# Position biases by an indirect DMA of rows in place of one-hot products

## The chip, the cores and the metric

The kernel runs on one core of a Trainium2 chip. The metric is the device time of one execution in microseconds (us); of several runs the median is given.

## The reference, cut to what matters

The program is two transformer blocks over 512 tokens of width 1024, in float32. The first has two layers with three kinds of attention (differential, forgetting, stick-breaking). The second has three branches (sparse attention with an index score, a gated recurrence, attention with low-rank keys) and a feed-forward part. The change touches one input of the sparse attention: a bias for each query, key and head, taken from a table of 32 buckets by the distance of two positions.

```python
def t5_bucket(dist):
    max_exact = REL_BUCKETS // 2
    d = jnp.maximum(dist, 0)
    dl = jnp.maximum(d, max_exact).astype(jnp.float32)
    large = max_exact + (jnp.log(dl / max_exact) / math.log(REL_MAX_DIST / max_exact)
                         * (REL_BUCKETS - max_exact)).astype(jnp.int32)
    large = jnp.minimum(large, REL_BUCKETS - 1)
    return jnp.where(d < max_exact, d, large)
...
        bias = rel_bias[t5_bucket(pb[:, :, None] - p_sel)]
        s = (jnp.einsum('bthd,btkd->bthk', qb, k_sel).astype(jnp.float32) * scale
             + jnp.moveaxis(bias, -1, 2).astype(jnp.float32))
```

The positions are read from an input; from a distance of 113 on all distances fall into the last bucket, and negative ones into the first.

## The kernel before, in words

A class `Net` issues everything; tiles are 128 partitions (P) by up to 512 columns (S), and the 512 tokens are four tiles (NT). Matrix products of full precision are done as three products of high and low parts: weights come by SP's queue into `wraw` (three buffers), ScalarE makes the high part `whi` (L189), VectorE the low part `wlo` (L190), and `mm3` (L197 to L199) issues the three products for each step into a bank `pj` of PSUM. A second kind of bank, `s`, has three buffers, which attention scores and the bias work share.

The biases do not depend on the activations. `bias2` computes them during the first layer of the first block and writes them to DRAM (`bias0` to `bias3`, one for each tile of queries); the sparse attention reads them back much later. It is a Python generator: each `yield` ends a step. `merge` and `merging` run one and a half of its steps for each step of the main sequence (`RATES[7]`, `RATES[8]`), first beside the projections of the values, queries and keys (four, two and two tiles), then beside two pairs of gate tiles; what is left is issued after them. The attention `att_b`, which is issued at a raised priority, runs beside the gates and what follows. A planner then orders the instructions of each engine by priority, program order and its own idea of when each is ready. Each engine, and each queue that issues DMAs (SP, POOL), then keeps that order.

`bias2` works by residues. Positions are taken modulo 256. For a residue of the query and one of the key the table `t5tab` gives the bias of their distance. For each head:

- `raw` reads, for each of the 256 key residues, a shifted row of the table from DRAM (SP's queue, L983) into a buffer `bo`, and `split` (L1032 ScalarE, L1033 VectorE) makes its high and low parts;
- products with the one-hot matrix `ok` of the keys' residues (L990) pick the columns: the result has a row for each of the 256 query residues and a column for each of the 512 keys, in two banks, each of which is split again into high and low parts `g`;
- for each tile of queries, products with the one-hot matrix `oq` of the queries' residues (L998) pick the rows, 128 to 512 columns wide, as keys after the tile are masked anyway;
- L1000 fills a tile `o` (again a buffer `bo`) with the bias of far distances, L1001 copies the picked values over it where the distance is near, and POOL writes it to DRAM (L1002).

`near` and `side`, masks that tell where a distance is near and which sign it has, are made once on VectorE, before the heads. The buffers are shared by tag: `bt` (six of 128x512), `bh` (four, the one-hot matrices) and `bo` (three, for table rows and outgoing biases alike). When `bias2` is done its memory goes to the buffers `lt`, in which the next projections' queries and keys are put (L643 to L646); the copies of L646 run on POOL.

Of the kernel before, what the change touches and what calls it, by code (L numbers as in the profile page):

```python
# [9 lines left out]
F32 = mybir.dt.float32  # L10
F32R = mybir.dt.float32r
# [3 lines left out]
ALU = mybir.AluOpType  # L15
# [4 lines left out]
P = 128  # L20
S = 512
# [12 lines left out]
class Net:  # L34
# [30 lines left out]
    def slot(self, dt=F32, shape=None):  # L65
        return self.u("t2k", shape or [P, S], self.nslot, dt)
# [846 lines left out]
    def bias2(self, pool):  # L913


        nc, a = self.nc, self.a
# [3 lines left out]
        hot = lambda: pool.tile([P, S], F32R, name=self.nm("bh"), tag="bh", bufs=4)  # L920
# [5 lines left out]
        col = self.t("b_col", [P, 4], 1)  # L926
# [26 lines left out]
        ok, oq = ([hot() for _ in range(2)] for _ in range(2))  # L953
        for j in range(2):
            nc.vector.tensor_scalar(ok[j], m, col[:, j:j + 1], None, op0=ALU.is_equal)
            nc.vector.tensor_scalar(oq[j], m, col[:, 2 + j:3 + j], None, op0=ALU.is_equal)
        yield
        ka = part(pi, ALU.arith_shift_right, 7, slot())
# [21 lines left out]
        for h in range(4):  # L980
            raw = pool.tile([P, 2, 256], F32, name=self.nm("bo"), tag="bo", bufs=3)
            x = tab[h]
            nc.sync.dma_start(raw, bass.AP(x.tensor, x.offset, [[1, P], [P, 2], [1, 256]]))  # L983
            f = self.split(raw.rearrange("p a b -> p (a b)"), slot)
            g = []
            for r in range(2):
                ps = self.p("s")
                for k, y in enumerate((0, 0, 1, 1)):
                    z = k % 2
                    nc.tensor.matmul(ps, lhsT=f[y][:, z * 256 + r * P:z * 256 + r * P + P], rhs=ok[z], start=k == 0, stop=k == 3)  # L990
                g.append(self.split(ps, slot))
            yield
            for i in range(NT):
                w = (i + 1) * P
                ps = self.p("s")[:, :w]
                for k, y in enumerate((0, 0, 1, 1)):
                    z = k % 2
                    nc.tensor.matmul(ps, lhsT=oq[z][:, i * P:w], rhs=g[z][y][:, :w], start=k == 0, stop=k == 3)  # L998
                o = pool.tile([P, S], F32, name=self.nm("bo"), tag="bo", bufs=3)[:, :w]
                nc.vector.tensor_scalar(o, side[i], te[:, 1, h:h + 1], te[:, 0, h:h + 1], op0=ALU.mult, op1=ALU.add)  # L1000
                nc.vector.copy_predicated(o, near[i].bitcast(U32), ps)  # L1001
# [706 lines left out]
def constants():  # L1708
# [36 lines left out]
    cc = np.arange(P, dtype=np.float32)[:, None] * [1, 1, -1, -1] + [0, 128, 255, 127]  # L1745
# [28 lines left out]
```

## Time and profile before

| | us |
|---|---|
| median of 3 runs | 1699.47 (1699.45 to 1704.51) |
| the profiled execution's own time | 1701.74 |
| its span in the profile | 1700.0 |
| TensorE busy | 1632.7 |
| VectorE busy | 1074.4 |
| ScalarE busy | 731.2 |
| GpSimd (POOL) busy | 124.9 |

The profile is of one execution. PE is TensorE's matmul, PEld its weight load, DVE is VectorE, ACT is ScalarE, POOL is GpSimd, SP is the engine that issues most DMAs; a letter q behind the name is that engine's instruction queue. Matmuls overlap each other in the record, so the busy time of a group is longer than the time in which the engine issues it; the distance between two starts gives the latter. A line such as L998 is the line of the kernel. In rows of waits the right side names what came last. The granted clock is the share of TensorE's full clock that the throttle let through.

### The profile page before, as it was taken

To read this page: it belongs to the slowest core of one execution; us is meant where nothing else is said; L and a number is where in the kernel's file an instruction comes from. 1 tells how busy PE (TensorE), PEld (TensorE's weight loads), DVE (VectorE), ACT (ScalarE), POOL (GpSimd) and SP (SyncE) were. 2 spreads that over 40 slices of the span, in tenths; PEclk is the share of its full clock that TensorE was granted. 3 is DMA by queue.
4 is the path that set the end of the run, shared out by engine and by line. 5 is a ranking of instruction groups with operands and counts; after the bars stand their busy time and mean duration, and the time that the engine had idled before them with its cause. 6 is when DMAs were issued, how large, how long until landed. Compare 5 with 4: busy or idle time off the path is not lost.

```text
span 1700.0 us, 24423 instructions
## 1 busy us (share of the span) xinstructions
PE 1632.7 (96%) x9384; PEld 1387.3 (82%) x9384; DVE 1074.4 (63%) x2363; ACT 731.2 (43%) x1484; POOL 124.9 (7%) x135
## 2 busy tenths in 40 slices
PE   7999999989999999799889999999999999999997
PEld 6877788878787979688778976788889988888997
DVE  7855878865657787855999996633445544443233
ACT  4434755434556643455443954522333322222222
POOL 2111000020000000201231000200000000000000
PEclk9999999999999999899999999999999999999999
DMA  6331123243121323432012230232523533332221
GB/s 219 109 101 46 38 87 91 84 125 100 38 75 36 115 74 109 133 89 89 13 33 69 64 102 4 90 100 87 173 81 125 186 99 99 99 97 90 96 89 65
DMA packets 140156, 153.79 MB, mean 90 GB/s; under 512 B 13908, under 2 KB 130916, under 8 KB 140040
## 3 DMA queue, kind: packets, MB, share of 16 engines
q1 hardware_dynamic: 134808, 139.24, 26.7%
q0 software_dynamic: 2368, 7.67, 1.3%
q10 hardware_dynamic: 2864, 5.32, 1.0%
q8 instruction: 74, 1.21, 0.3%
q14 instruction: 42, 0.34, 0.1%
HBM read 139.36 MB, written 13.12 MB: 90 GB/s over the span
## 4 chain that ended last, share of the span: by engine, by line
PE 79%; DVE 14%; ACT 3%; DMA 2%; issue 2%; POOL 0%; ACTq 0%; DVEq 0%; SPq 0%; POOLq 0%
PE pj L197 19%; PE pj L199 19%; PE pj L198 19%; PE pv L1022 3%; PE s L199 2%; PE s L198 2%; PE s L197 2%; PE tr L666 2%; PE s L652 1%; PE s L769 1%; PE s L653 1%; DVE ixs L1239 1%; DVE wlo L190 1%; ACT whi L189 1%; DVE tok L286 1%
## 5 line engine op out<-in xcount | busy, mean ns | idle before, releaser
L198 PE MATMUL pj<-hTl,whi 128*128 128x512 f32 (+1 forms) x1136 | 440.6, 388 | 0.0
L197 PE MATMUL pj<-hTh,whi 128*128 128x512 f32 (+1 forms) x1136 | 440.5, 388 | 0.0
L199 PE MATMUL pj<-hTh,wlo 128*128 128x512 f32 (+1 forms) x1136 | 440.0, 388 | 0.0
L190 DVE TENSOR_TENSOR wlo<-wraw,whi 128x1024 fp32r<-128x1024 f32 (+1 forms) x235 | 269.3, 1152 | 236.5 <-ACT whi L189 234.8
L189 ACT CAST whi<-wraw 128x1024 fp32r<-128x1024 f32 (+3 forms) x245 | 237.2, 982 | 354.9 <-PE pj L198 188.8
L197 PEld LDWEIGHTS pj<-hTh,whi 128*128 128x128 f32 x1136 | 213.8, 188 | 45.0 <-issue 6.3
L198 PEld LDWEIGHTS pj<-hTl,whi 128*128 128x128 f32 x1136 | 213.8, 188 | 43.4 <-issue 4.4
L199 PEld LDWEIGHTS pj<-hTh,wlo 128*128 128x128 f32 x1136 | 213.8, 188 | 43.2 <-issue 3.8
L199 PE MATMUL pj<-whi,hTl 128*128 128x256 f32 (+2 forms) x416 | 121.7, 295 | 2.4 <-DVE hTl L263 2.4
L197 PE MATMUL pj<-whi,hTh 128*128 128x256 f32 (+2 forms) x416 | 120.9, 292 | 0.9 <-ACT hTh L262 0.9
L198 PE MATMUL pj<-wlo,hTh 128*128 128x256 f32 (+2 forms) x416 | 121.0, 292 | 0.0
L198 PE MATMUL pj<-wlo,t2k 128*128 128x256 f32 x304 | 85.7, 282 | 0.0
L199 PE MATMUL pj<-whi,t2k 128*128 128x256 f32 x304 | 85.5, 281 | 0.0
L197 PE MATMUL pj<-whi,t2k 128*128 128x256 f32 x304 | 85.3, 281 | 0.0
L199 PEld LDWEIGHTS pj<-whi,hTl 128*128 128x128 f32 x416 | 81.6, 197 | 3.5 <-DVE hTl L263 3.1
L197 PEld LDWEIGHTS pj<-whi,hTh 128*128 128x128 f32 x416 | 81.9, 197 | 2.0 <-ACT hTh L262 1.8
L198 PEld LDWEIGHTS pj<-wlo,hTh 128*128 128x128 f32 x416 | 82.1, 198 | 0.4 <-DVE wlo L190 0.2
L199 PE MATMUL s<-whi,t2k 128*128 128x256 f32 x264 | 73.8, 280 | 0.0
L197 PE MATMUL s<-whi,t2k 128*128 128x256 f32 x264 | 73.8, 280 | 0.0
L198 PE MATMUL s<-wlo,t2k 128*128 128x256 f32 x264 | 73.8, 280 | 0.0
L669 ACT COPY wa<-tr 128x128 f32<-128x128 f32 (+3 forms) x96 | 40.7, 424 | 59.3 <-PE tr L666 57.7
L657 DVE CUSTOM_DVE_ANT_0 wa<-s,mask 128x128 f32<-128x128 f32 (+3 forms) x112 | 52.3, 485 | 14.2 <-PE tr L666 7.6
(441 smaller groups left out, 3081.3 us busy)
## 6 DMA issues: line engine op xcount, KB each, us to landing
wraw<-in_w_in_dram SPq DMA_DIRECT2D x112, 512.0 KB, 3.8
wraw<-in_w_ffn_gate_dram SPq DMA_DIRECT2D x22, 512.0 KB, 4.6
wraw<-in_w_ffn_up_dram SPq DMA_DIRECT2D x22, 512.0 KB, 4.7
wraw<-in_w_ffn_down_dram SPq DMA_DIRECT2D x16, 512.0 KB, 4.4
tok<-hres SPq DMA_DIRECT2D x12, 512.0 KB, 7.4
wraw<-in_w_out_dram SPq DMA_DIRECT2D x12, 512.0 KB, 3.5
hres<-tok SPq DMA_DIRECT2D x12, 512.0 KB, 2.9
wraw<-in_w_out_dram SPq DMA_DIRECT2D x8, 384.0 KB, 3.0
```

Of the source, the lines that this page charges most:

```text
L189: nc.scalar.copy(hi[:, ka:kb], raw)
L190: (eng or nc.vector).tensor_sub(lo[:, ka:kb], raw, hi[:, ka:kb])
L197: nc.tensor.matmul(out, lhsT=wh(k), rhs=xh(k), start=start and k == 0, stop=False)
L198: nc.tensor.matmul(out, lhsT=wh(k), rhs=xl(k), start=False, stop=False)
L199: nc.tensor.matmul(out, lhsT=wl(k), rhs=xh(k), start=False, stop=stop and k == nk - 1)
L286: nc.vector.scalar_tensor_tensor(y, y, mv[:, 2:3], g[half], op0=ALU.add, op1=ALU.mult)
L652: nc.tensor.matmul(sc, lhsT=stacked[:, rows], rhs=twice[hh][:, cols], start=True, stop=False)
L653: return nc.tensor.matmul(sc, lhsT=stacked[:, rows], rhs=twice[2 + hh][:, cols], start=False, stop=stop)
L657: self.nc.vector.tensor_tensor_reduce(p[:, :w], sc[:, :w], self.maskw[:, S - w:] if mask is None else mask, scale=1.0, scalar=3e38, op0=AL ...
L666: x = nc.tensor.transpose(pt[:, j, :], src[:, j * P:(j + 1) * P], self.ident)
L669: nc.scalar.copy(dst[:, :n, :], pt[:, :n, :])
L1022: x = self.nc.tensor.matmul(out, lhsT=l, rhs=r, start=k == 0, stop=k == i)
```

## The change

The one-hot matrix `oq` of the queries and its products (L998) go, and so does the second split. The 256 rows of all four heads are copied from PSUM by ScalarE as they are and written to a DRAM tile `rows` (256 x 4 x 512) by SP's queue. For this, the four heads' first products are issued ahead of the `near` and `side` masks. For each tile of queries, an indirect DMA on POOL's queue then fetches, for each of its 128 queries, that query's row of 4 x 512 values (8 KB) into a buffer `bq`, of which there is one. The predicated copies read from it. The loop over heads is now inside the loop over tiles. Row indices are two operations on small integers: 255 minus the position modulo 256.

```diff
--- before.py
+++ after.py
@@ -913,17 +913,19 @@
     def bias2(self, pool):
 
 
+
         nc, a = self.nc, self.a
         U32 = mybir.dt.uint32
         self.bias = [self.dr.tile([P, 4, (i + 1) * P], F32, name=f"bias{i}") for i in range(NT)]
         slot = lambda dt=F32, shape=None: pool.tile(shape or [P, S], dt, name=self.nm("bt"), tag="bt", bufs=6)
-        hot = lambda: pool.tile([P, S], F32R, name=self.nm("bh"), tag="bh", bufs=4)
+        hot = lambda: pool.tile([P, S], F32R, name=self.nm("bh"), tag="bh", bufs=2)
+        rows = self.dr.tile([256, 4, S], F32, name="t5rows")
         pos = a["positions_2"]
         pi = slot(I32)
         nc.sync.dma_start(pi, pos.broadcast_to([P, S]))
         qi = self.t("b_qi", [P, 3, NT], 1, I32)
         nc.sync.dma_start(qi[:, 0], pos[0].rearrange("(t p) -> p t", p=P))
-        col = self.t("b_col", [P, 4], 1)
+        col = self.t("b_col", [P, 2], 1)
         nc.sync.dma_start(col, a["c_col"])
         rb = self.t("b_rb", [32, 4], 1)
         nc.sync.dma_start(rb, a["rel_bias_2"])
@@ -950,11 +952,26 @@
             return out
 
         m = part(pi, ALU.bitwise_and, 255, slot())
-        ok, oq = ([hot() for _ in range(2)] for _ in range(2))
+        ok = [hot() for _ in range(2)]
         for j in range(2):
             nc.vector.tensor_scalar(ok[j], m, col[:, j:j + 1], None, op0=ALU.is_equal)
-            nc.vector.tensor_scalar(oq[j], m, col[:, 2 + j:3 + j], None, op0=ALU.is_equal)
+        nc.vector.tensor_single_scalar(qi[:, 1], qi[:, 0], 255, op=ALU.bitwise_and)
+        nc.vector.tensor_scalar(qi[:, 2], qi[:, 1], -1.0, 255.0, op0=ALU.mult, op1=ALU.add)
         yield
+        for h in range(4):
+            raw = pool.tile([P, 2, 256], F32, name=self.nm("bo"), tag="bo", bufs=3)
+            x = tab[h]
+            nc.sync.dma_start(raw, bass.AP(x.tensor, x.offset, [[1, P], [P, 2], [1, 256]]))
+            f = self.split(raw.rearrange("p a b -> p (a b)"), slot)
+            for r in range(2):
+                ps = self.p("s")
+                for k, y in enumerate((0, 0, 1, 1)):
+                    z = k % 2
+                    nc.tensor.matmul(ps, lhsT=f[y][:, z * 256 + r * P:z * 256 + r * P + P], rhs=ok[z], start=k == 0, stop=k == 3)
+                g = slot()
+                nc.scalar.copy(g, ps)
+                nc.sync.dma_start(rows[r * P:(r + 1) * P, h, :], g)
+            yield
         ka = part(pi, ALU.arith_shift_right, 7, slot())
         kr = part(pi, ALU.bitwise_and, 127, slot())
         qf = self.t("b_qf", [P, 2, NT], 1)
@@ -977,28 +994,15 @@
             near.append(n)
             side.append(s)
             yield
-        for h in range(4):
-            raw = pool.tile([P, 2, 256], F32, name=self.nm("bo"), tag="bo", bufs=3)
-            x = tab[h]
-            nc.sync.dma_start(raw, bass.AP(x.tensor, x.offset, [[1, P], [P, 2], [1, 256]]))
-            f = self.split(raw.rearrange("p a b -> p (a b)"), slot)
-            g = []
-            for r in range(2):
-                ps = self.p("s")
-                for k, y in enumerate((0, 0, 1, 1)):
-                    z = k % 2
-                    nc.tensor.matmul(ps, lhsT=f[y][:, z * 256 + r * P:z * 256 + r * P + P], rhs=ok[z], start=k == 0, stop=k == 3)
-                g.append(self.split(ps, slot))
-            yield
-            for i in range(NT):
-                w = (i + 1) * P
-                ps = self.p("s")[:, :w]
-                for k, y in enumerate((0, 0, 1, 1)):
-                    z = k % 2
-                    nc.tensor.matmul(ps, lhsT=oq[z][:, i * P:w], rhs=g[z][y][:, :w], start=k == 0, stop=k == 3)
+        for i in range(NT):
+            w = (i + 1) * P
+            ps = pool.tile([P, 4 * S], F32, name=self.nm("bq"), tag="bq")
+            nc.gpsimd.indirect_dma_start(out=ps, out_offset=None, in_=rows.rearrange("r h k -> r (h k)"),
+                                         in_offset=bass.IndirectOffsetOnAxis(ap=qi[:, 2, i:i + 1].bitcast(U32), axis=0))
+            for h in range(4):
                 o = pool.tile([P, S], F32, name=self.nm("bo"), tag="bo", bufs=3)[:, :w]
                 nc.vector.tensor_scalar(o, side[i], te[:, 1, h:h + 1], te[:, 0, h:h + 1], op0=ALU.mult, op1=ALU.add)
-                nc.vector.copy_predicated(o, near[i].bitcast(U32), ps)
+                nc.vector.copy_predicated(o, near[i].bitcast(U32), ps[:, h * S:h * S + w])
                 nc.gpsimd.dma_start(self.bias[i][:, h, :], o)
                 yield
 
@@ -1742,7 +1746,7 @@
     for j in range(S):
         d = (255 - j + 128) % 256 - 128
         t5[sum(max(d, 0) >= x for x in T5_THR) - 1, j] = 1.0
-    cc = np.arange(P, dtype=np.float32)[:, None] * [1, 1, -1, -1] + [0, 128, 255, 127]
+    cc = np.arange(P, dtype=np.float32)[:, None] + [0, 128]
 
     cs = np.zeros((16, 2), np.float32)
     cs[:8, 0], cs[8:, 0], cs[8:, 1] = 1.0, -1.0, 1.0
```

## Rows read from the trace of the kernel before

**Rows 1.** The page: busy time by engine, and the chain that ended last.

```profile
PE 1632.7 (96%) x9384; PEld 1387.3 (82%) x9384; DVE 1074.4 (63%) x2363; ACT 731.2 (43%) x1484; POOL 124.9 (7%) x135
...
PE 79%; DVE 14%; ACT 3%; DMA 2%; issue 2%; POOL 0%; ACTq 0%; DVEq 0%; SPq 0%; POOLq 0%
```

**Rows 2.** Stretches: length; PE, PEld, DVE, ACT, POOL busy; clock; DMA share; GB/s.

```profile
50.00:60.00 10.00, 9.34 (x46) 7.58 (x45) 10.00 (x28) 4.08 (x6) 0.00 (x0) 1.00 0.12 41
...
120.00:130.00 10.00, 7.09 (x37) 5.48 (x35) 3.42 (x8) 0.93 (x3) 2.16 (x4) 1.00 0.53 141
130.00:140.00 10.00, 9.11 (x43) 7.26 (x43) 5.99 (x15) 3.16 (x7) 1.62 (x3) 0.83 0.11 40
...
150.00:160.00 10.00, 10.00 (x56) 7.38 (x55) 6.86 (x19) 6.39 (x16) 1.66 (x2) 1.00 0.01 2
```

**Rows 3.** TensorE in order of time: start, duration, line, tiles, form, count.

```profile
64.85 1.08 PE L998 MATMUL s<-bt,bh 128*128 128x128 f32 x8
65.77 0.40 PE L197 MATMUL pj<-hTh,whi 128*128 128x512 f32 x1
...
71.27 0.86 PE L998 MATMUL s<-bt,bh 128*128 128x384 f32 x4
71.96 0.40 PE L197 MATMUL pj<-hTh,whi 128*128 128x512 f32 x1
...
77.46 1.09 PE L998 MATMUL s<-bt,bh 128*128 128x512 f32 x4
78.38 2.00 PE L990 MATMUL s<-bh,bt 128*128 128x512 f32 x8
80.22 0.40 PE L197 MATMUL pj<-hTh,whi 128*128 128x512 f32 x1
```

**Rows 4.** TensorE in order of time, 108 to 136 us; idle before in brackets.

```profile
108.24 0.41 PE L666 MATMUL tr<-ident,wa 128*128 128x128 f32 x2 [0.67 <-DVE wa L1008]
...
126.70 0.39 PE L199 MATMUL pj<-hTh,wlo 128*128 128x512 f32 x1
130.89 3.03 PE L990 MATMUL s<-bh,bt 128*128 128x512 f32 x8 [3.80 <-ACT bt L1032]
133.72 0.63 PE L197 MATMUL pj<-hTh,whi 128*128 128x512 f32 x1
...
135.22 1.94 PE L998 MATMUL s<-bt,bh 128*128 128x128 f32 x12
```

**Rows 5.** The chain that ended last, 110 to 146 us: start, length, what.

```profile
121.05 4.22 DMA bias<-bo
125.34 4.86 DMA bo<-t5tab
```

**Rows 6.** Waits from 20 to 150 us: total, times, longest, all in us.

```profile
ACT bt L1032 <- DMA bo<-t5tab: 14.5, 3, 7.9
...
DVE bo L1000 <- DMA bias<-bo: 8.1, 5, 3.4
```

**Rows 7.** VectorE by line and form, 20 to 145 us: busy, mean ns, idle.

```profile
L1033 DVE TENSOR_TENSOR bt<-s,bt 128x512 fp32r<-128x512 f32 x8 | 5.4, 689 | 1.7 <-ACT bt L1032 1.6
```

**Rows 8.** DMA issues, whole span: count, KB each, median us to landing.

```profile
wraw<-in_w_in_dram SPq DMA_DIRECT2D x112, 512.0 KB, 3.8
...
tok<-hres SPq DMA_DIRECT2D x12, 512.0 KB, 7.4
...
bias<-bo POOLq DMA_DIRECT2D x4, 256.0 KB, 2.4
```

**Rows 9.** SP's queue in order of time, from 45 to 72 us.

```profile
45.18 3.29 SPq L187 DMA_DIRECT2D wraw<-in_w_in_dram  x2
...
59.66 10.35 SPq L187 DMA_DIRECT2D wraw<-in_w_in_dram  x4
```

**Rows 10.** POOL in order of time, from 82 to 149 us.

```profile
82.74 0.77 POOL L646 CAST t2k<-t2k 64x512 fp32r<-64x512 f32 x1
...
148.01 0.86 POOL L646 CAST lt<-lt 64x512 fp32r<-64x512 f32 x1 [4.97 <-DVE st L1007]
```

## The prediction, made before the change was run

> **What bounds the kernel now.** I read the page first, for who holds the end. TensorE is busy 1632.7 us of a span of 1700.0 us and the chain that ended last runs 79% through it [rows 1]; the reader is to see that an edit pays here only if TensorE issues less or waits less. The profiled execution took 1701.74 us, 1.74 us more than its span, and lies 2.27 us above the median of 1699.47 us; I make the sum against 1701.74 and take off 2.27 at the end.
>
> Then the stretches of ten microseconds in which the bias work lies, from about 50 to 146 us. TensorE is in use nearly throughout, except from 120 to 140 us, where it loses some 3 us of use and the granted clock falls to 0.83 [rows 2]. The stretch from 150 to 160 us has no bias matmuls left, only attention and projections, and TensorE is still at 10.00 of 10: when the bias work goes, other work is there to move up. That is why I count removed issue time fully. A busy figure overlaps pipelined matmuls, so I take issue time from TensorE's list of instructions, as the distance from one start to the next [rows 3]. Last I followed the hole after 126 us in the same list [rows 4] and in the chain [rows 5].
>
> **What is removed, term one: 64 one-hot products at L998.** Each head has four of each width 128, 256, 384 and 512. The eight of the two small widths start at 64.85 and the next instruction at 65.77: 0.92 us. The four of 384 take 71.27 to 71.96: 0.69 us. The four of 512 take 77.46 to 78.38: 0.92 us [rows 3]. A head costs 2.53 us, four heads 10.1 us, at the full clock. The 32 products of L990 (1.84 us a head, 78.38 to 80.22 [rows 3]) stay: they only move.
>
> **Term two: the hole after 126 us.** The last projection matmul starts at 126.70 and takes the 0.23 us of its kind; the next instruction on TensorE starts at 130.89 [rows 4]: 3.96 us lost. The chain says what was late: a bias write of 4.22 us had to land before a buffer `bo` came free, then the last head's table rows had to be read, 4.86 us [rows 5]. Table rows and outgoing biases share three `bo` buffers, and the fourth head's table is asked for after three heads' biases. After the change all four tables are loaded before any bias is written, so no bias write stands ahead of one. The hole goes: 4.0 us.
>
> **Term three: the clock after the hole.** The eight products of the last head take 130.89 to 133.72, 2.83 us in place of 1.84; what follows to 135.22 is three projection matmuls and one small product, 1.50 us in place of 3 x 0.23 + 0.115 = 0.81 [rows 3, 4]. After the idle stretch the engine ran on the lower level (1.2 GHz) for a while, which the 0.83 of that window shows [rows 2]. 1.0 + 0.7 = 1.7 us go with the hole.
>
> Sum of gains: 10.1 + 4.0 + 1.7 = 15.8 us.
>
> **What leaves VectorE and what stays.** Eight low-part subtractions (L1033, 0.69 us each [rows 7]) and two compares go from VectorE, some 6 us; two operations on 128x4 integers come. ScalarE's eight casts become eight copies of the same tile, no change. VectorE is not the bound where the hole lies and after it (3.4 to 6.9 of 10 from 120 us on [rows 2]), so I count nothing; the cover is its idle time, and without it 6 us of VectorE would be worth 6 us more gain, not a loss. The predicated copies read SBUF in place of PSUM: nothing for it either, as they stay on VectorE beside idle time.
>
> **What is moved.** The four heads' L990 products now follow the second, third and fourth value tile, with heads two and three back to back. Each needs its table read, the ScalarE cast, the VectorE subtraction and room in the six `bt` buffers, of which `pi` now keeps one until all heads are done. A head holds two split buffers until its products are done and two row buffers until its row writes have landed. From below this costs nothing, when the split of the last head is ready in time; from above it is the row-write rival below. I take 1.5 us, about one cast and one subtraction in the open between the two adjacent heads.
>
> **What is added.** Eight row writes of 256 KB on SP's queue: the bias writes of that size land in a median of 2.4 us [rows 8]. SP waits with weight loads for free buffers, and a row write behind such a load waits with it. Four gathers on POOL's queue, 1 MB each, one landing buffer for all. The trace has no indirect transfer. Loads of 512 KB landed in 3.8 us (weights) and 7.4 us (rows of the residual from DRAM) [rows 8]; twice these are 7.6 and 14.8 us, and I take 11, between them, since a gathered row of 8 KB is closer in kind to the residual's rows but nothing says how the queue deals with single rows. It could also be nearly hidden or worse. No matmul waits for a gather. Who does: the predicated copies on VectorE, and behind them, in order, the weight splits and softmax steps; on POOL the copies at L646 for attention's keys. With the rows complete at about 60 us and four rounds of 11 + 3 us the last bias is out by about 116 us, and the first copy into the buffers that take over this memory comes at 148.01 now [rows 10], about 132 after a gain of 16. That is the cover; gathers of up to 15 us fit it. For VectorE waits that reach TensorE I take 1 us. The nearest pattern is in the waits of before: VectorE already waits 8.1 us in five times for bias writes, and no hole on TensorE answers to it [rows 6]. The 6 MB more of traffic stand against windows with 0.11 to 0.53 of the DMA engines busy [rows 2]: nothing.
>
> Net: 15.8 - 1.5 - 1.0 = 13.3 us. 1701.74 - 13.3 = 1688.4, less 2.27: **1686 us**.
>
> **A rule against the change.** The rows show POOL copying keys for attention one at a time, the last of the first four at 82.74 in 0.77 us [rows 10]: a gather ahead of it in POOL's order delays it by as long as the gather holds the engine. The Trainium skill, GPSIMD Engine Reference, section Performance pitfalls for Q7 kernels, gives about 102 cycles for each small read such as one per gather index. By that an estimate for 128 indices at that page's 1.2 GHz is 10.9 us of POOL for a gather, before any data moves. No run here shows whether the indirect transfer pays that. The sum with the rows' prices does not need it; its result is the slower rival.
>
> **Rivals.**
>
> *Row writes held on SP.* SP issued two weight loads from 45.18 to 48.47 and the next one only at 59.66, held by a buffer [rows 9]. If the first heads' row writes stand behind that load, their `bt` buffers come free 11 us later, the last heads' splits wait, and TensorE sits in order before L990. Back from 64.85 [rows 3] by two query tiles of 24 x 0.23 us and one head, the value tiles end at about 52 now, so with three heads among them the third is done at about 57.5. The most it costs is 59.66 + 2.4 + 1.3 (cast, subtraction) - 57.5 = 5.9 us. Against it: the planner that orders the queues places a transfer when it thinks it is ready. Time, with this in place of the 1.5: 1686 - 1.5 + 5.9 = about 1690.
>
> *No gain.* The attention steps between could be bound by their own chain of softmax operations, so that removed products only turn into waiting. For it: TensorE waited 0.67 us for a softmax step at 108.24 [rows 4]. Against it: full use at 150 to 160 us without any bias matmul [rows 2]. It would leave the hole's 4 us or less: 1695.5 to 1699.5. The same result comes if the planner, given other work here, orders later stages a little worse.
>
> *VectorE stands behind the gathers: slower.* If the planner thinks the gathers shorter than they are, each first predicated copy stops VectorE. The price per wait is shown by ScalarE's longest wait for a table, 7.9 us [rows 6], which cost TensorE 4.0 us: a wait costs what exceeds 3.9 us. Four gathers waited for in full at 14.8 us cost 4 x 10.9 = 43.6 us: 1699.5 - 15.8 + 43.6 = 1727 us. It decides from waits of 7.9 us each (no gain) and makes the kernel slower by 5 us from 9.2 us each. POOL held by the index reads gives the same, with the copies of L646 late in place of VectorE. Against it: VectorE has other work only from its own program order, and row and gather come early against their use.
>
> **How the numbers follow.** Forecast 0.62, row writes held 0.14, no gain 0.14, slower 0.10. About 0.3% (5.1 us) is what a measurement of this kernel can tell from no change. Faster by more than that: the forecast and the held writes, less 0.01 for their tails, 0.75; within: no gain and these, 0.15; slower: 0.10. Range: with none of the 2.5 us given back the time is 1683.7; the 0.67 us before L666 could go as well, and the order of the rest could fall better by a hole of the size taken for each of the two costs, 2.5 us: low end 1680. High end 1697, which takes in the held writes and the better half of no gain. Outside are the slower case and the rest of no gain.
>
> **What would show it.** TensorE: no L998, 64 matmuls fewer, no idle time of 3 us or more between 50 and 140 us, and the granted clock at 1.00 there. The first key copies of L646's late buffers some 13 to 16 us earlier. On VectorE, waits for the gather summing to little; on POOL, the last bias write before about 130 us. Wrong would be: a hole on TensorE before L990, named with ScalarE or a row write; VectorE idle for several microseconds before a predicated copy with weight splits queued behind it; or the later stages longer by more than 2 us at equal work.

## The result, and the profile after

The changed kernel takes 1684.01 us, median of four runs (1681.91 to 1684.75), beside 1700.12 us for the kernel before on the same chip (1699.45 to 1704.51, four runs): ratio 0.9898, 95% interval 0.9886 to 0.9910. That is 16.1 us less by the medians and about 17 by the ratio. The time predicted was 1686, from 1680 to 1697. A second measurement on another chip gave 0.9904 (0.9891 to 0.9917). The profiled execution took 1684.35 us, with a span of 1682.6.

The page of the changed kernel, busy time by engine and the chain that ended last, beside [rows 1]:

```profile
PE 1619.7 (96%) x9320; PEld 1377.5 (82%) x9320; DVE 1067.2 (63%) x2355; ACT 730.1 (43%) x1484; POOL 129.2 (8%) x139
...
PE 78%; DVE 13%; ACT 2%; issue 2%; DMA 1%; POOL 0%; ACTq 0%; POOLq 0%
```

TensorE has 64 matmuls fewer (9384 to 9320) and is 13.0 us less busy; ScalarE is the same to 1.1 us. TensorE still holds the end: the chain runs 78% through it.

Stretches of the changed kernel, columns as in [rows 2]; then TensorE's waits from 20 to 160 us (total, times, longest):

```profile
50.00:60.00 10.00, 9.24 (x50) 7.28 (x49) 3.74 (x4) 5.43 (x9) 0.00 (x0) 1.00 0.55 183
...
80.00:90.00 10.00, 8.34 (x43) 6.47 (x43) 9.38 (x27) 5.99 (x15) 4.01 (x6) 1.00 0.53 143
...
120.00:130.00 10.00, 10.00 (x58) 8.12 (x57) 6.58 (x12) 2.50 (x6) 1.65 (x3) 1.00 0.71 239
130.00:140.00 10.00, 10.00 (x46) 8.29 (x45) 4.08 (x5) 3.08 (x4) 0.90 (x3) 1.00 0.38 110
```

```profile
PE s L652 <- DVE t2k L645: 1.6, 2, 1.2
PE tr L258 <- DVE rs_i L221: 0.8, 1, 0.8
PE s L970 <- ACT bt L1036: 0.8, 1, 0.8
```

The hole of 120 to 140 us is gone, and so is the low clock behind it [rows 2, 4]. New gaps stand at 54 us (0.8, before a moved table head, L970) and at 81 to 85 us (1.2 and 0.5, the layer's keys, at a time when VectorE is at 9.38 of 10). Ahead of the first of them ScalarE waited for a row write to leave its buffer, and the cast of the table rows stood behind that:

```profile
53.33 0.59 ACT L972 COPY bt<-s 128x512 f32<-128x512 f32 x1 [2.76 <-DMA t5rows<-bt]
53.81 0.62 ACT L1036 CAST bt<-bo 128x512 fp32r<-128x512 f32 x1
```

Instructions on the landing buffer `bq` of the changed kernel: counts with min, median and max in ns, what their engine waited for, and who waited for them:

```profile
L1000 POOL DMA_INDIRECT bq<-t5rows,b_qi x4: 998/1006/1030, 67.6 to 116.5; - x4
...
  DMA bq<-t5rows,b_qi: 0.4, 1
...
DMA to landing us min/median/max: 5.6/5.6/5.7
```

A gather holds POOL for 1.0 us and its megabyte lands 5.6 us after the issue; VectorE waited 0.4 us for all four together.

Where the time was saved is seen with one mark: the forget gates' first sums (L769), an instruction of the next stage that both kernels have. First of the kernel before, then of the one after, both from the tile's list (x count, min/median/max ns, first and last start):

```profile
L769 PE MATMUL s<-ch,nones x48: 277/282/340, 175.3 to 546.7; 128*128 128x256 f32 x40, 128*128 128x384 f32 x8
```

```profile
L769 PE MATMUL s<-ch,nones x48: 277/282/340, 158.0 to 529.6; 128*128 128x256 f32 x40, 128*128 128x384 f32 x8
```

The first start comes 17.3 us earlier, the last one 17.1, and the span is 17.4 shorter: to within 0.2 us everything was saved ahead of the mark, and the later stages moved as one block.

The stretch up to this mark can be taken apart for any kernel: TensorE's idle time (length less busy, over windows of ten microseconds), the time at less than the full clock (length times one less the granted clock), and the rest, which is work at the full clock. A clock given in hundredths makes the middle term uncertain by some tenths. Ahead of the mark all kernels have the same matmuls to within two, but for the 64 products and for six projection matmuls more in e3, so the last column can be compared.

| kernel | mark, us | idle | low clock | rest |
|---|---|---|---|---|
| before | 175.3 | 16.0 | 3.4 | 155.9 |
| after, first profile | 158.0 | 13.0 | 0.0 | 145.0 |
| after, second profile (e9) | 158.4 | 12.5 | 1.8 | 144.1 |
| e1 own table buffers | 169.9 | 13.3 | 0.0 | 156.6 |
| e2 unread products | 178.3 | 21.5 | 3.4 | 153.4 |
| e3 gathers twice | 169.7 | 18.3 | 3.4 | 148.0 |
| e4 masks first | 162.9 | 15.1 | 1.7 | 146.1 |
| e5 before, no products | 159.7 | 13.8 | 1.7 | 144.2 |
| e6 e5 with own buffers | 160.1 | 12.9 | 3.5 | 143.7 |
| e7 ten buffers | 163.0 | 16.0 | 1.7 | 145.3 |
| e8 masks first, keys on ScalarE | 161.2 | 12.6 | 3.4 | 145.2 |
| e10 masks between heads | 163.3 | 14.8 | 3.4 | 145.1 |
| e11 e10, keys on ScalarE | 161.9 | 13.6 | 3.4 | 145.0 |
| e12 plain reads | 157.9 | 13.9 | 0.0 | 144.0 |

Before to after: 10.9 us less work, 3.0 us less idle, 3.4 us less at the low clock.

### The profile page after: what moved, and what is told of

Same layout as the page of the kernel before. It is cut to its first block, busy times and chain, and to the rows that moved or that the text cites. A ratio compares the mean times of both kernels' runs of the same rounds, so it can differ in the third digit from the quotient of the medians.

```text
span 1682.6 us, 24320 instructions
## 1 busy us (share of the span) xinstructions
PE 1619.7 (96%) x9320; PEld 1377.5 (82%) x9320; DVE 1067.2 (63%) x2355; ACT 730.1 (43%) x1484; POOL 129.2 (8%) x139
## 4 chain that ended last, share of the span: by engine, by line
PE 78%; DVE 13%; ACT 2%; issue 2%; DMA 1%; POOL 0%; ACTq 0%; POOLq 0%
PE pj L198 19%; PE pj L197 19%; PE pj L199 19%; PE pv L1026 3%; PE s L199 2%; PE s L197 2%; PE s L198 2%; PE tr L666 2%; PE s L769 1%; PE s L652 1%; PE s L653 1%; DVE ixs L1243 1%; DVE wlo L190 1%; PE pv L780 1%; DVE tok L286 1%
## 5 line engine op out<-in xcount | busy, mean ns | idle before, releaser
L197 PE MATMUL pj<-hTh,whi 128*128 128x512 f32 (+1 forms) x1136 | 440.8, 388 | 0.0
L199 PE MATMUL pj<-hTh,wlo 128*128 128x512 f32 (+1 forms) x1136 | 439.9, 388 | 0.4 <-DVE wlo L190 0.4
L197 PEld LDWEIGHTS pj<-hTh,whi 128*128 128x128 f32 x1136 | 213.7, 188 | 45.6 <-issue 6.8
L199 PEld LDWEIGHTS pj<-hTh,wlo 128*128 128x128 f32 x1136 | 213.6, 188 | 43.2 <-issue 3.8
L199 PE MATMUL pj<-whi,hTl 128*128 128x256 f32 (+2 forms) x416 | 121.9, 294 | 1.6 <-DVE hTl L263 1.5
L197 PE MATMUL pj<-whi,hTh 128*128 128x256 f32 (+2 forms) x416 | 120.9, 292 | 0.9 <-ACT hTh L262 0.7
L197 PE MATMUL pj<-whi,t2k 128*128 128x256 f32 x304 | 85.6, 281 | 0.0
L199 PE MATMUL pj<-whi,t2k 128*128 128x256 f32 x304 | 85.5, 281 | 0.0
L199 PEld LDWEIGHTS pj<-whi,hTl 128*128 128x128 f32 x416 | 81.5, 196 | 2.9 <-DVE hTl L263 2.6
L197 PEld LDWEIGHTS pj<-whi,hTh 128*128 128x128 f32 x416 | 81.9, 197 | 2.0 <-ACT hTh L262 1.7
L199 PE MATMUL s<-whi,t2k 128*128 128x256 f32 x264 | 73.9, 280 | 0.0
L197 PE MATMUL s<-whi,t2k 128*128 128x256 f32 x264 | 73.9, 280 | 0.0
```

The lines of the kernel that those rows point to most:

```text
L197: nc.tensor.matmul(out, lhsT=wh(k), rhs=xh(k), start=start and k == 0, stop=False)
L199: nc.tensor.matmul(out, lhsT=wl(k), rhs=xh(k), start=False, stop=stop and k == nk - 1)
```

## The experiments

The theory from the prediction: the gain is the removed products on TensorE, plus a hole that went with the shared `bo` buffers; the gathers are covered. Rivals: the gain comes from the wait alone; the products were hidden; the gathers cost something that the gain outweighs. The kernels of e1 to e4 ran on one chip, those of e5 to e8 on a second, e9 to e12 on a third, each beside the kernel before (medians 1700.64, 1701.82 and 1700.97 us). The changed kernel lay 16.1 and 16.4 us below the kernel before in its two measurements; "over after" says by how much a run's distance to the kernel before on its own chip falls short of that.

**e1: the kernel before, table rows in buffers of their own.**

```diff
-            raw = pool.tile([P, 2, 256], F32, name=self.nm("bo"), tag="bo", bufs=3)
+            raw = pool.tile([P, 2, 256], F32, name=self.nm("br"), tag="br", bufs=2)
```

> The kernel before with one edit: the table rows of each head get two buffers of their own, so that they no longer wait for a bias write to leave a buffer; products and everything else stay. Theory (the gain is issue time of the removed products, plus the hole at the last head's table, plus the low clock after it): the hole and the clock go alone, -4.0 - 1.7 = -5.7 us, ratio about 0.9966. Rival A (the whole gain comes from having the tables early, the products were hidden in waits): near the changed kernel, -14 to -16 us. Rival B (the hole only shows where TensorE lacks work and opens elsewhere): within 1.5 us of before.

Measured: 1695.3 us, ratio 0.9972 (0.9961 to 0.9983), 5.3 us less by the medians. TensorE's waits from 20 to 160 us:

```profile
PE s L990 <- DVE bt L1033: 1.8, 1, 1.8
PE s L652 <- DVE bo L1001: 0.8, 1, 0.8
```

The hole of 3.8 us named with ScalarE is not there any more. The wait of 1.8 for the subtraction is another one: it stands before the first head, at 57.7 us, where the kernel before waited 0.7. The table gives idle -2.6 and low clock -3.4, with work up by 0.7. Of the low clock 1.7 lies between 20 and 40 us, far ahead of the edit, and is no gain of it (see e9). By the medians, a mere change of buffers is worth about a third of the whole gain, as the theory had it.

**e2: the changed kernel with 64 products put back, which nobody reads.**

```diff
                 nc.vector.tensor_scalar(o, side[i], te[:, 1, h:h + 1], te[:, 0, h:h + 1], op0=ALU.mult, op1=ALU.add)
+                px = self.p("s")[:, :w]
+                for k in range(4):
+                    nc.tensor.matmul(px, lhsT=ok[k % 2][:, i * P:w], rhs=ok[k % 2][:, :w], start=k == 0, stop=k == 3)
                 nc.vector.copy_predicated(o, near[i].bitcast(U32), ps[:, h * S:h * S + w])
```

> The changed kernel with 64 products of the removed shapes put back at the place of the predicated copies, from the keys' one-hot matrix with itself; nothing reads them. Theory: TensorE's issue time comes back, +10.1 us over the changed kernel, ratio to before about 0.996. Rival A (hidden products): within 1.5 us of the changed kernel, ratio about 0.990.

Measured: 1707.17 us, ratio 1.0041 (1.0028 to 1.0054): some 23 us over after, more than twice the 10.1. The table splits them: work +8.4, idle +8.5, low clock +3.4. The work is near the theory: added up over all 64 products, the time from each start to the next instruction's start is 10.8 us here, 10.7 in the kernel before and 11.0 in e1. For the rest, TensorE's longest wait from 20 to 190 us, the stretches, and VectorE in order of time with the idle before in brackets:

```profile
PE s L713 <- DVE g L699: 6.6, 1, 6.6
```

```profile
90.00:100.00 10.00, 3.35 (x12) 2.41 (x12) 5.94 (x15) 0.55 (x3) 3.99 (x6) 0.75 0.47 146
100.00:110.00 10.00, 9.51 (x46) 7.59 (x45) 6.58 (x19) 3.82 (x9) 2.19 (x4) 0.91 0.49 174
```

```profile
91.50 1.53 DVE L1008 COPY_PREDICATED bo<-b_n,bq 128x256 f32<-128x256 uint32 x3 [2.63 <-DMA bq<-t5rows,b_qi]
94.50 0.41 DVE L1004 TENSOR_SCALAR bo<-b_s,b_te 128x256 f32<-128x256 bf16 x1 [1.47 <-DMA bias<-bo]
...
96.84 0.47 DVE L698 TENSOR_SCALAR wa<-wa,sel 16x512 f32<-16x512 f32 x1
97.45 0.74 DVE L699 SCALAR_TENSOR_TENSOR g<-s,sel,wa 16x512 fp32r<-16x512 f32 x1
98.12 0.46 DVE L1004 TENSOR_SCALAR bo<-b_s,b_te 128x384 f32<-128x384 bf16 x1
```

VectorE stood 2.63 us for the second gather and 1.47 for a bias write, with L698 and L699 behind in its order, and TensorE waited 6.6 us for L699 before L713. In the changed kernel VectorE waits 0.4 us for gathers. Who waited for the instructions on `bq` in this kernel, in us and times:

```profile
  DVE bo L1008: 7.5, 3
  POOL t2k L646: 5.7, 1
```

A key copy on POOL (L646) is among them, and the bias write that VectorE waited 1.47 us for went out on POOL right behind that copy. So the prediction's slower rival is a real mechanism of this kernel: products in this place make the order put the copies where a gather has not landed yet.

**e3: every gather twice.**

```diff
-            nc.gpsimd.indirect_dma_start(out=ps, out_offset=None, in_=rows.rearrange("r h k -> r (h k)"),
-                                         in_offset=bass.IndirectOffsetOnAxis(ap=qi[:, 2, i:i + 1].bitcast(U32), axis=0))
+            for _ in range(2):
+                nc.gpsimd.indirect_dma_start(out=ps, out_offset=None, in_=rows.rearrange("r h k -> r (h k)"),
+                                             in_offset=bass.IndirectOffsetOnAxis(ap=qi[:, 2, i:i + 1].bitcast(U32), axis=0))
```

> The changed kernel with each gather issued twice into the same buffer, the second after the first has landed: 4 MB more, and each round of four heads some 6.6 us longer (1.0 us issue and 5.6 us to landing in the changed kernel's trace). Theory: no matmul waits for a gather, so the time stays within 1.5 us of the changed kernel, as the last bias write moves from 131 to about 150 us and the new users of that memory come at 140; a part of the next projections' copies may then wait, at most some 10 us. Rival C (VectorE stands in order behind the gathers and TensorE behind it): +6 to +26 us.

Measured: 1695.54 us, ratio 0.9970 (0.9958 to 0.9982), about 11 us over after. The theory's 1.5 us fell; the rival's bounds hold it, though VectorE is only a part of the cause, as the waits show. The second gather of a pair waits until the first has landed (17.4 us in four times), so the rounds are longer by a whole landing. TensorE's waits from 20 to 165 us:

```profile
PE s L653 <- POOL t2k L646: 2.6, 1, 2.6
PE pj L197 <- DVE lt L644: 2.2, 1, 2.2
PE s L652 <- DVE t2k L645: 2.2, 1, 2.2
```

A key copy on POOL waits 5.5 us for a gather here, and that is the 2.6 of TensorE. The copy reads nothing of the gather, but in the built program it stands behind a wait for the gather's landing. The kernel before has no gather to wait for; the changed kernel has the same wait, but there that landing (issued at 87.43, so 93.0 us) lies ahead of the copy (95.15). Why the program has this wait was not followed up.

**e4: the changed kernel, table heads behind the masks again.** The block of the four heads goes back behind the loop that makes `near` and `side`:

```diff
         yield
-        for h in range(4):
-            raw = pool.tile([P, 2, 256], F32, name=self.nm("bo"), tag="bo", bufs=3)
...
         ka = part(pi, ALU.arith_shift_right, 7, slot())
...
             side.append(s)
             yield
+        for h in range(4):
+            raw = pool.tile([P, 2, 256], F32, name=self.nm("bo"), tag="bo", bufs=3)
```

> The changed kernel with the near and side masks issued ahead of the four heads' first products, as before the change. Theory (the two holes of 1.2 and 0.5 us before attention's first scores come from VectorE, on which the masks stand between 64 and 78 us): these holes go, -1.7 us, and the one before the first head's products comes back, +0.7 us: 0 to -2 us against the changed kernel. Rival D (the early heads are what the gain rests on, since gathers and biases get out in time): +2 us or more.

Measured: 1687.81 us, ratio 0.9927 (0.9916 to 0.9939), 3.3 to 3.6 us over after: the move is not neutral, the rival holds. TensorE's waits from 20 to 165 us:

```profile
PE s L653 <- POOL t2k L646: 2.4, 1, 2.4
PE pj L199 <- DVE wlo L190: 2.1, 1, 2.1
```

The first gather goes out at 84.3 in place of 67.6, and a key copy on POOL then meets a gather that is still under way (it waits 4.1 us).

**e5: the kernel before without the products.**

```diff
-                ps = self.p("s")[:, :w]
-                for k, y in enumerate((0, 0, 1, 1)):
-                    z = k % 2
-                    nc.tensor.matmul(ps, lhsT=oq[z][:, i * P:w], rhs=g[z][y][:, :w], start=k == 0, stop=k == 3)
+                ps = g[i % 2][0][:, :w].bitcast(F32)
```

> The kernel before, without the 64 one-hot products at L998; the predicated copy reads the first split part of the keys' table from SBUF instead, so the picking of each query's row is left out and the biases are other numbers. Nothing else is changed: the row tables, masks, bias writes and the wait at 127 to 131 us stay. Theory (the products were work of TensorE that nothing hid, 2.53 us a head): about 10.1 us faster than the kernel before, ratio 0.994, and the wait of some 4 us before the last head's table products is still there or somewhat longer, as TensorE comes to it earlier. Rival A (the products filled gaps of TensorE, and the gain of the change came from the wait alone): within 1.5 us of the kernel before.

Measured: 1684.03 us, ratio 0.9893 (0.9878 to 0.9908): 17.8 us less by the medians, not 10.1, and the wait did not stay. TensorE's waits from 20 to 175 us, then two lines of the chain that ended last:

```profile
PE s L990 <- DVE bt L1030: 1.4, 1, 1.4
PE s L990 <- ACT bt L1029: 1.1, 1, 1.1
```

```profile
115.61 2.03 DMA bias<-bo
117.78 5.16 DMA bo<-t5tab
```

The first of the two waits is the first head's again (0.7 in the kernel before); the second is what is left of the hole. The chain is the one of [rows 5], a bias write and then the last table read, but the read is asked for 7.6 us earlier (117.78 against 125.34) and TensorE stops 1.1 us in place of 3.8. In the kernel before, the products stand in this chain, just ahead of [rows 5], and its waits from 20 to 150 us have the copies waiting for products:

```profile
119.80 0.48 PE s L998 x4
120.31 0.45 DVE bo L1001
```

```profile
DVE bo L1001 <- PE s L998: 5.1, 6, 2.5
```

The products are not all of it: 2.2 of the 7.6 us are the shorter landing of the bias write (2.03 against 4.22), for which no run shows a cause. Up to the mark e5 is 15.6 us ahead of the kernel before; 1.6 more come between the first and the last of the sums.

**e6: e5 with the table rows in buffers of their own**, the diffs of e5 and e1 together.

> The same as the kernel before without the products at L998 (the picking of each query's row is left out), and the tables of the biases read into two buffers of their own, so that no table read waits for a bias write. Theory (the whole gain is the products and the wait, and the gathers cost TensorE nothing): 10.1 us and the 4.8 us that own buffers gave by themselves, 14.9 us faster, ratio 0.991, up to 15.8 by the prediction's sum; within 2 us of the changed kernel. Rival (the changed kernel gains something more, from the move of the table products or from the earlier bias writes): 3 us or more slower than the changed kernel, ratio above 0.9915.

Measured: 1683.82 us, ratio 0.9889 (0.9874 to 0.9905). Own buffers, worth 5 us in e1, add nothing that can be measured here: they close what e5 left of the hole (1.1 us), and the first head's wait grows from 1.4 to 1.9 us. The theory holds: the kernel lies 1.6 to 1.9 us below the changed one, so what the rows and gathers add to the time shows as no more than that.

**e7: the changed kernel with ten `bt` buffers** (`bufs=6` to `bufs=10`).

> The changed kernel with ten buffers instead of six for the rows on their way to DRAM and the masks, so that the masks' slots don't wait for the row writes. Theory (the two new gaps of TensorE at 81 and 85 us, 1.65 us in sum, come from VectorE doing the held-back masks late): about 1.7 us faster than the changed kernel, VectorE's windows of 70 to 100 us less full, no gap above 0.5 us in them. Rival (the masks compete with the layer's own VectorE work whenever they run): within 0.5 us of the changed kernel, gaps of the same sum at another place.

Measured: 1687.48 us, ratio 0.9914 (0.9900 to 0.9928), 2 us over after. The theory fell: the gap at the keys is 1.8 us in place of 1.6. The masks had not been held by row writes: in both kernels VectorE starts on them right behind the last splits and the head scores (64.1 us after, 70.9 here). And the four extra buffers delayed something else: three of the four table reads went out at 32.8 us in the changed kernel, and all four only from 48.7 on here, behind a load of the bucket table at 39.0; TensorE stood 2.0 us before a head (L970). That load came late with the larger buffers; why was not followed up.

**e8: e4 with the layer's second key copies (L646) on ScalarE.**

```diff
-            nc.gpsimd.tensor_copy(u[rest], u[own])
+            (nc.scalar.copy if self.kact else nc.gpsimd.tensor_copy)(u[rest], u[own])
```

(`kact` is true for the keys of this layer only.)

> The changed kernel with the four table heads moved behind the masks again (as e4), and the second key copies of the layer beside them (L646) on ScalarE instead of GpSimd, so that they are not queued behind the gathers. Theory (e4 lost 4 us because a key copy on GpSimd waited until a gather had landed: a gap of 2.4 us and the lower clock behind it): 3 to 5 us faster than e4, about the changed kernel's time, ratio 0.990, and no gap before L653. Rival (e4 lost because the table heads came later, and VectorE with them): within 1 us of e4, ratio 0.993, with the gap before L653 replaced by another.

Measured: 1687.05 us, ratio 0.9905 (0.9890 to 0.9920), against 0.9927 for e4. The gap of 2.4 us before L653 is gone, and idle time falls by 2.5 us in the table; of TensorE's waits from 20 to 175 us only the other one is left with more than 0.5 us, 0.4 us longer than in e4 (the edit shifts the line numbers by one):

```profile
PE pj L200 <- DVE wlo L191: 2.6, 1, 2.6
```

By the medians it is 1.9 us faster than e4, where 3 to 5 were expected: the low clock behind L653 is gone, but in this execution it is there between 20 and 40 us (1.7) and behind the gap of 2.6 (1.7). The gap's cause is shown; the size can't be told from one profile of each.

**e9: the changed kernel again**, beside the last three.

> The changed kernel once more, beside the next three on the same chip and against the same runs of the kernel before: ratio 0.990, TensorE idle about 13 us before the forget gates' sums begin, of which 2.4 us lie at 54 and at 81 to 85 us. All theories expect the same of it; what differs from its first profile is the size of what two executions of one kernel differ by, up to 2 us, in the low clock of the stretch of 20 to 40 us above all.

Measured: 1684.57 us, ratio 0.9904 (0.9891 to 0.9917). The profile differs from the first where expected: 1.8 us at the low clock, nearly all of it between 30 and 40 us (clock 0.85), where the first profile had 1.00. The kernel before has it there too. First the kernel before, then e9:

```profile
30.00:40.00 10.00, 9.93 (x72) 9.68 (x72) 8.88 (x34) 2.66 (x6) 1.10 (x2) 0.86 0.69 217
```

```profile
30.00:40.00 10.00, 10.00 (x74) 9.95 (x74) 8.60 (x33) 3.13 (x6) 1.06 (x2) 0.85 0.87 251
```

**e10: the masks made between the table heads**, and the keys' block numbers in buffers of their own. The mask loop becomes a function `mask(i)`, called after a head's row writes:

```diff
                 nc.sync.dma_start(rows[r * P:(r + 1) * P, h, :], g)
             yield
+            for i in ((0, 1), (2,), (3,), ())[h]:
+                mask(i)
+                yield
```

> The changed kernel with the masks made between the four table heads (two after the first head, one after the second, one after the third) and the keys' block numbers kept as bf16 in buffers of their own. Theory (VectorE stands 9 us for the heads' splits between 46 and 63 us and then has the masks in a block from 64 to 78 us, behind which the key rotation comes late): the gaps of TensorE at 81 and 85 us, 1.65 us in sum, shrink to under 0.5 us, about 1.5 us faster than the changed kernel, ratio 0.989. Rival (the masks then delay the heads' splits or the weights' low parts, L190, as in the kernel with all masks first): a gap of 2 us or more at 50 to 70 us instead, the same time as the changed kernel or up to 4 us slower.

Measured: 1687.33 us, ratio 0.9922 (0.9910 to 0.9933), 2.8 us more than e9. TensorE's waits from 20 to 160 us:

```profile
PE s L653 <- POOL t2k L646: 1.9, 1, 1.9
PE s L993 <- ACT bt L1040: 1.7, 1, 1.7
...
PE s L652 <- DVE t2k L645: 0.4, 1, 0.4
```

The gap at the keys shrinks to 0.4 as the theory had it, but the masks delay the heads (1.7 before L993), the first gather goes out at 85.8, and a key copy on POOL waits for a gather again.

**e11: e10 with the key copies on ScalarE**, the diffs of e10 and e8 together.

> As the run with the masks between the heads, and the second key copies of the layer beside them (L646) on ScalarE instead of GpSimd, so that none of them stands behind a gather. Theory: if a key copy on GpSimd waits in the run with the masks between the heads, this one is 2 to 4 us faster than that; if none does, the same within 1 us. It should be the fastest kernel of all, ratio 0.988 to 0.989. Rival (ScalarE is then late with the weights' high parts): 1 us or more slower than the run without this edit.

Measured: 1685.25 us, ratio 0.9908 (0.9895 to 0.9921), 2.1 us less than e10, whose gap of 1.9 before L653 is gone; TensorE's largest wait is the head's (2.8 before L996). So it gets back to the changed kernel and not below it. No version beat it by more than the intervals.

**e12: a plain read of the same bytes for each gather.**

```diff
-            nc.gpsimd.indirect_dma_start(out=ps, out_offset=None, in_=rows.rearrange("r h k -> r (h k)"),
-                                         in_offset=bass.IndirectOffsetOnAxis(ap=qi[:, 2, i:i + 1].bitcast(U32), axis=0))
+            nc.gpsimd.dma_start(ps, rows[:P].rearrange("r h k -> r (h k)"))
```

> The changed kernel with each gather replaced by a plain DMA of the first 128 rows of the table, from the same queue and of the same bytes; each query's own row is not picked, so the biases are other numbers. Theory (a gather costs this kernel nothing that reaches TensorE: 1.0 us on GpSimd and 5.6 us to its landing, both covered): the same time as the changed kernel within 1 us, and a landing of 4 to 6 us. Rival (the indirect form is dear, and the changed kernel pays for it): 2 us or more faster than the changed kernel.

Measured: 1683.52 us, ratio 0.9903 (0.9890 to 0.9916), e9's 0.9904 to within anything that can be told. From the list of `bq`:

```profile
L1000 POOL DMA_DIRECT2D bq<-t5rows x4: 542/548/551, 66.0 to 116.1; - x4
...
DMA to landing us min/median/max: 5.1/5.2/5.6
```

The indirect form costs 0.46 us more of POOL and 0.4 us more to land, and none of it reaches the end.

## Why the prediction was right, step by step

The forecast case came, with its mechanism: the products go, the hole and its low clock go, the gathers stay covered. The time is 2 us below 1686 and inside the range.

- **Term one, 10.1 us.** The work at the full clock fell by 10.9 us (11.8 by e9). The unread products of e2 brought 8.4, and without the products the kernel before lost 11.7 (e5) or, with own buffers, 12.9 (e6 against e1). The forecast lies within these; the products were not hidden. Reckoning all four heads from one left out little: added up over all 64, the distances between starts are 10.7 us in the kernel before. What the further 1 to 2 us in e5 and e6 are is not settled: one profile of each does not tell that apart from the differences between executions.
- **Terms two and three, 4.0 and 1.7 us.** Both are there: the hole is gone and the clock is 1.00 behind it. But they were no cost of the buffers alone. Own buffers take the hole away (e1), and leaving out the products takes most of it (3.8 to 1.1 us, e5); doing both gives no more time (e6). The cause named, a bias write and then a table read, was right, and the products stood ahead of it in the chain, as the copies waited for them. The sum was right as the change does both. Whoever had added e1's 5.3 us and e5's 17.8 us would have promised 23.
- **What leaves VectorE: nothing.** Right in the sum, and the cover named is there to see: VectorE is not full where the hole lay (6.58 and 4.08 of 10).
- **The moved heads, 1.5 us.** One gap of 0.8 us before a head, behind a row write. Moving the heads ahead of the masks also sets when the gathers go out, and so keeps them clear of the key copies: without it e4 loses 3.3 to 3.6 us. The prediction had not seen this use of the move.
- **The gathers, 1.0 us.** Landing was taken at 11 us and took 5.6; each of the two nearest rows was twice a load of 512 KB, and a megabyte from POOL's queue did not take twice. The wait that reached TensorE is 1.6 us at 81 to 85 us, but it is for VectorE's key rotation, which shares a full VectorE with masks, weight splits and the first copies. e12 shows that it is no price of the gathers: the gap is 1.6 us there too. Against this, the gaps of 0.66 and 0.67 us of before are gone. New gaps less those is 1.1 us net, where 2.5 were given back.
- **The cover of the gathers.** Here the working was wrong and two errors met. Rounds of 11 + 3 us from about 60 us on were to have the last bias out by 116. The gathers went out at 67.6, 87.4, 102.1 and 116.5: each landed in half of 11 us, but what followed in a round took 9 to 14 us and not 3, so the last bias write went out at 130.9, and the first copy into the memory taken over came 7.7 us earlier than before, not 13 to 16. These two signs of the prediction missed. By the prediction's own reckoning the cover shrank from 16 us to 9, and it held. In e3, with longer rounds, it ends: ScalarE's first write into that memory (L643) waits 3.9 us for the last bias write, and the 2.2 us of TensorE's L197 are behind it.

```profile
130.93 0.54 POOL L1006 DMA_DIRECT2D bias<-bo  x1 [5.38 <-DVE bo L1005]
...
140.32 0.79 POOL L646 CAST lt<-lt 64x512 fp32r<-64x512 f32 x1 [8.50 <-DVE lt L644]
```

- **The remainder.** 10.9 + 3.0 + 3.4 = 17.3. Of the 3.4, 1.7 is term three; the other 1.7 is the low clock between 20 and 40 us in the profile of before, which e9 has too and which so belongs to the execution and not to the change.
- **The rivals.** Row writes on SP: a buffer was indeed held by a row write (one of the eight took 6.2 us to land where 2.4 was taken, and ScalarE waited 2.8 us for it); that cost TensorE 0.8 us, not 5.9. No gain: refuted by e5, where only products go and all of the gain comes. VectorE behind the gathers: did not happen in the changed kernel, but e2 shows it at 6.6 us of TensorE, and e3, e4 and e10 show POOL's variant, a key copy that waits 3.6 to 5.5 us for a gather and costs TensorE 1.9 to 2.6. The prediction's argument against them (row and gather come early against their use) is what decides. In e4 and e10 it tips with the first gather's start, 84 us and later in place of 67.6. In e2 and e3 the first gather goes out as early as in the changed kernel (65.6 and 67.5), and it is the second one that has not landed when the key copy is due: 84.1 us against 87.4 in the changed kernel for e2, whose copy comes earlier still, and a doubled round for e3. That the changed kernel keeps clear of this is an order that the prediction argued for without a number; there was luck in it.
- **POOL held by the index reads.** A gather held POOL for 1.0 us. The rule weighed in the prediction (the Trainium skill, GPSIMD Engine Reference, section Performance pitfalls for Q7 kernels) would have made it 10.9 us as an estimate; the trace does not agree, and the measurement decides: a price for small reads by a program on those cores is not the price of an indirect DMA's indices here.

## What to carry to other kernels

Costs on one engine's path don't add when one feeds the other: before summing "work removed" and "wait removed", follow the wait back past its last releaser and see whether the removed work is in the chain ahead of it. An edit that turns matmuls into transfers is free only as long as the consumers of the transfer are ordered after its landing; look for who shares an in-order engine with the transfer's issue or with its consumers (here a key copy on POOL and a head score on VectorE), and issue the transfer early: making it shorter gained nothing here (e12). Moving work into an idle stretch of VectorE helped the place aimed at and hurt the next, both times it was tried (e4, e10).

## What the runs showed of the hardware

- An indirect DMA of 128 rows of 8 KB (1 MB) from POOL's queue took 1.0 us of POOL and landed in 5.6 us in the changed kernel (up to 7.6 in e2); a plain one of the same bytes took 0.55 us and 5.2 us (e12). The Trainium skill, DMA: Bandwidth & Descriptors, section Anatomy of one DMA, fits a transfer from GpSimd as 2.0 us and its bytes over 436 KB for each microsecond, which gives an estimate of 4.4 us for a megabyte; both measured landings, from the issue on, are above it by about 1 us.
- A gap of TensorE costs more than its length when the clock falls behind it. The gaps of 2.4 us in e4 and of 1.9 us in e10 before L653 each came with a granted clock of 0.83 from 100 to 110 us, 1.7 us more; the gaps of 81 to 85 us in the changed kernel (1.2 and 0.5) came with 1.00, and so did e4's 2.1 us before L199, while e8's 2.6 us at the same place came with 0.83 from 50 to 60 us. The runs don't tell what decides.
- Two executions of one kernel differed by the low clock of an early stretch: 1.00 or 0.85 between 30 and 40 us, so 1.5 us.
